# A hybrid decoder trunk on one core: the scheduler's order taken from its detailed timing model instead of its simple one

## The chip, the cores and the metric

The kernel runs on one core of a Trainium2 chip. The metric is device time in microseconds of one execution of the whole program; lower is better. The kernel before was timed three times: 1619.57, 1621.16 and 1629.75 us, so its median is 1621.16 us. The execution that was profiled took 1613.0 us, of which the span from the first to the last instruction is 1610.9 us.

## The reference

One layer of a decoder, applied to a prompt of 2048 tokens and to 8 sequences of 8 new tokens, all in 32-bit floats. In outline:

```python
xn = rms_norm(x, norm_g);  p = xn @ w_in              # 1024 -> 4224 columns
# convolution branch (512 wide): h, bg, cg, gc are columns of p
u = cg * h;  z = causal width-3 convolution of u over positions
y_conv = bg * z * silu(gc)
# RWKV-7 branch (8 heads of 64): r, k, v, low-rank decay and learning-rate inputs, gate
pr = pr + mu_shift * (previous position's pr - pr)
decay = exp(-c * sigmoid(w0 + tanh(wl) @ w_dec2));  a = sigmoid(a0 + al @ w_a2)
kk = normalised(k * k_k);  k = k * (1 + (a - 1) * k_a)
# per token: S = S diag(w) + (S(-kk)) (kk*a)^T + v k^T ;  o = S r
y_rwkv = (group_norm(o) + bonus) * silu(gr)
out = rms_norm(x + concat(y_conv, y_rwkv) @ w_out, final_norm_g)
```

Besides the outputs of both sets of tokens, the last convolution rows, the last normalised row and the final matrix states are returned.

## The kernel before, in words

**Stages.** The prompt is handled in two halves of 1024 tokens; the 64 sample tokens ride along with the first half. Each half first normalises and transposes its rows (`xprep`, lines 211 to 289) and then runs four stages, one for each pair of heads, so there are eight stages (the loop at line 932). After them `out_weights` and `out_tile` (lines 883 to 924) multiply by the output weights and store the result in 17 row blocks.

**A stage.** `rwkv_pair` (line 430) projects the columns r, k, v and the gate of the pair and prepares the operands of the recurrence on VectorE (DVE), ScalarE (ACT) and GpSimd (POOL). `inverse` (line 640) inverts small triangular matrices: the matrices go to DRAM and come back in another layout (`na<-dn`), 31 dependent pairs of DVE operations substitute through them (`subst`, line 614, tiles `sub` and `xi`), the result is stored (`dx<-xi`, line 669) and 12 DMAs bring it back into the tile `AB` (line 678); a DVE transpose (line 680, tile `na`) and small matmuls into the PSUM tile `cx` follow. `wkv` (line 726) then walks through the half in 16 chunks of 64 tokens, each depending on the one before. In a chunk TensorE and DVE take turns: matmuls into `ca`, the copy `xs` (line 741), matmuls into `ca`, the scaling `u` (line 751), matmuls into `cb`, and the new state into `sv` (line 120). `conv_group` (line 329) projects the four column groups of the convolution branch and works on them; it depends on nothing of the recurrence.

**Projections.** Every projection of 128 columns (`project`, line 309) is a series of 24 matmuls for each of three token blocks, all into the PSUM tile `pj`: the weights and the rows are split into a high and a low part (`split`, line 205: a copy on ACT, a subtraction on DVE or POOL), and three products are summed. In the first half the weights are split on POOL (`wl<-wr,wh`) and stored; in the second half they are loaded back split.

**What sets the order.** The kernel is written for a tile framework. The Python code records all instructions, in the order in which the functions are called, with what each one reads and writes. When the context closes, a scheduler replays the recorded instructions on a timing model of the core. Each time an engine comes free in that model, it is given the earliest recorded instruction among those whose inputs and buffers the model holds ready. The order found in this way is written into each engine's queue, and on the chip every engine works through its queue in exactly that order, waiting wherever the next instruction isn't ready. No order is written out by hand; the record order serves as the priority, and because `conv_group` and the next stage's `rwkv_pair` are recorded after `wkv`, their matmuls fill the places at which the model finds the chain of a stage waiting. Buffers of a tile pool are also handed out in the scheduler's order.

The last lines of the kernel open the context and record the program; the timing model is chosen there.

## Time and profile before

| what | us |
|---|---|
| median of three runs | 1621.16 |
| lowest and highest run | 1619.57, 1629.75 |
| the profiled execution: its own time | 1613.0 |
| its span, first to last instruction | 1610.9 |
| TensorE matmul (PE) busy | 1512.1 |
| TensorE weight load (PEld) busy | 1265.4 |
| VectorE (DVE) busy | 1011.3 |
| ScalarE (ACT) busy | 616.2 |
| GpSimd (POOL) busy | 289.6 |

The profile names an instruction by its engine, the line that recorded it, and the tiles that it writes and reads (`out<-in`). Line 129 is the helper that records every matmul and line 117 the one for copies, lines 120 and 123 those for DVE operations on two inputs, so for them the tile tells which step it is. SP is the queue that issues most DMAs. Idle time of an engine is put down to whatever was ready last before the instruction that ended it. PE's ends of matmuls are modelled. PEclk is the granted clock of TensorE as a share of 2.4 GHz: 1.00 is that level, 0.5 is 1.2 GHz, and a value between them is a mean over a stretch with both.

### The profile page before, as it was taken

The page shows a single profiled execution, that of the slowest core. Times are in us where ns is not written, and L with a number is a line of the kernel's source. Part 1 is how long each engine was busy: PE and PEld are TensorE (multiplying, and loading weights), DVE is VectorE, ACT ScalarE, POOL GpSimd, SP SyncE. Part 2 cuts the span into 40 slices and gives each one's busy share as a digit, 9 for nine tenths or more (in the row PEclk, how much of TensorE's full clock was granted, in tenths as well). Part 3 has the DMA queues.
Part 4 walks back from the last instruction along what each step waited for, and adds up shares of the span by engine and source line. Part 5 has one row for each costly group of instructions (what it writes and reads, how often), then busy time and mean ns, then how long its engine had stood idle before and what let it go on. Part 6 is the DMA issues. An engine that isn't in the chain of part 4 may idle for free.

```text
span 1610.9 us, 29335 instructions
## 1 busy us (share of the span) xinstructions
PE 1512.1 (94%) x11088; PEld 1265.4 (79%) x11088; DVE 1011.3 (63%) x3101; ACT 616.2 (38%) x1591; POOL 289.6 (18%) x395
## 2 busy tenths in 40 slices
PE   4999999999999999989999999999999999899997
PEld 4989778887788777877789678877897788567885
DVE  6377458765687458784586358545864578466544
ACT  6443346324542354344541354135313543342221
POOL 3134103311133112320022002200220022000000
PEclk9989999899999998999999899999999999899999
DMA  7323412342043213441124112411241145414441
GB/s 241 118 83 110 137 49 74 108 122 78 20 136 113 95 50 112 140 125 61 36 73 125 42 36 66 135 39 37 77 127 38 34 118 155 133 62 137 143 137 53
DMA packets 121967, 151.90 MB, mean 94 GB/s; under 512 B 62617, under 2 KB 86681, under 8 KB 121826
## 3 DMA queue, kind: packets, MB, share of 16 engines
q1 hardware_dynamic: 107024, 104.53, 21.2%
q0 software_dynamic: 9536, 34.64, 6.8%
q10 hardware_dynamic: 5266, 10.86, 1.9%
q8 instruction: 88, 1.44, 0.4%
q14 instruction: 53, 0.43, 0.1%
HBM read 92.60 MB, written 57.35 MB: 93 GB/s over the span
## 4 chain that ended last, share of the span: by engine, by line
PE 63%; DVE 23%; issue 5%; DMA 5%; ACT 2%; POOL 1%; SPq 1%; ACTq 0%; DVEq 0%; POOLq 0%
PE pj L129 41%; PE ca L129 5%; PE ax L129 5%; DVE sub L123 5%; PE cb L129 4%; DVE xi L123 4%; DVE hp L123 2%; PE oo L129 2%; PE cx L129 2%; DVE hp L120 1%; PE cx L703 1%; DVE bk L123 1%; DVE t L120 1%; DMA dx<-xi 1%; DMA AB<-dx 1%
## 5 line engine op out<-in xcount | busy, mean ns | idle before, releaser
L129 PE MATMUL pj<-xh,wh 128*128 128x384 f32 (+3 forms) x1856 | 655.4, 354 | 18.0 <-DVE hp L123 13.8
L129 PE MATMUL pj<-xl,wh 128*128 128x384 f32 (+3 forms) x1856 | 652.8, 352 | 2.7 <-POOL xl L207 2.1
L129 PE MATMUL pj<-xh,wl 128*128 128x384 f32 (+3 forms) x1856 | 650.9, 351 | 0.8 <-DMA wl<-wsp 0.8
L129 PEld LDWEIGHTS pj<-xh,wh 128*128 128x128 f32 x1856 | 356.7, 192 | 50.1 <-DVE hp L123 11.5
L129 PEld LDWEIGHTS pj<-xl,wh 128*128 128x128 f32 x1856 | 356.8, 192 | 31.7 <-POOL xl L207 3.0
L129 PEld LDWEIGHTS pj<-xh,wl 128*128 128x128 f32 x1856 | 355.8, 192 | 27.3 <-issue 1.7
L117 ACT ACTIVATE tS<-sv,wc 64x64 f32<-64x64 f32 x256 | 88.0, 344 | 114.8 <-DVE sv L120 94.2
L207 POOL TENSOR_TENSOR wl<-wr,wh 128x512 fp32r<-128x512 f32 x66 | 87.8, 1342 | 193.4 <-ACT wh L117 190.0
L120 DVE SCALAR_TENSOR_TENSOR sv<-cb,wc,tS 64x64 f32<-64x64 f32 x240 | 68.0, 283 | 62.6 <-PE cb L129 56.1
L129 PE MATMUL ax<-L,bk 64*128 64x128 f32 x528 | 79.1, 298 | 20.9 <-DVE bk L123 11.2
L129 PEld LDWEIGHTS ax<-L,bk 64*128 64x128 f32 x528 | 66.1, 197 | 37.9 <-issue 23.6
L123 DVE TENSOR_TENSOR sub<-xi,na 128x126 f32<-128x126 f32 (+22 forms) x248 | 81.5, 329 | 16.5 <-DMA na<-dn 9.7
L117 ACT ACTIVATE t<-pj,prm 128x384 f32<-128x384 f32 (+3 forms) x170 | 68.8, 433 | 54.5 <-PE pj L129 53.4
L751 DVE TENSOR_SCALAR u<-ca,Q 128x64 f32<-128x64 f32 x128 | 36.2, 283 | 82.3 <-PE ca L129 82.1
L531 POOL TENSOR_TENSOR bk<-t,t 64x384 f32<-64x384 f32 (+2 forms) x56 | 58.3, 1041 | 155.3 <-ACT t L503 72.9
L123 DVE TENSOR_TENSOR xi<-xi,sub 128x126 f32<-128x126 f32 (+22 forms) x248 | 77.6, 313 | 7.1
L117 ACT ACTIVATE wh<-wr 128x512 fp32r<-128x512 f32 x66 | 40.5, 626 | 92.0 <-PE pj L129 73.1
L129 PEld LDWEIGHTS ca<-sv,L 128*64 128x64 f32 x528 | 43.3, 134 | 37.2 <-DVE sv L120 12.8
L129 PE MATMUL ca<-sv,L 128*64 128x64 f32 x528 | 67.8, 245 | 0.1
L741 DVE COPY xs<-ca 128x64 f32<-128x64 f32 x128 | 28.7, 224 | 60.4 <-PE ca L129 50.6
L298 POOL DMA_DIRECT2D wh<-wsp x33 | 18.6, 565 | 254.1 <-PE pj L129 216.7
L123 DVE TENSOR_TENSOR hp<-pj,hp 128x512 f32<-128x512 f32 (+1 forms) x34 | 23.4, 689 | 62.6 <-PE pj L129 62.2
(207 smaller groups left out, 2057.4 us busy)
## 6 DMA issues: line engine op xcount, KB each, us to landing
wr<-in_w_in SPq DMA_DIRECT2D x66, 256.0 KB, 3.7
wsp<-wh SPq DMA_DIRECT2D x33, 512.0 KB, 3.1
wsp<-wl SPq DMA_DIRECT2D x33, 512.0 KB, 3.5
wh<-wsp POOLq DMA_DIRECT2D x33, 512.0 KB, 3.6
wl<-wsp POOLq DMA_DIRECT2D x33, 512.0 KB, 4.8
hp<-in_x_prompt SPq DMA_DIRECT2D x28, 512.0 KB, 4.1
la<-yd SPq DMA_DIRECT2D x16, 512.0 KB, 4.0
out_y_p<-hp ACTq DMA_DIRECT2D x16, 512.0 KB, 2.6
```

What stands on the lines that cost most here:

```text
L117: act.activation(out=out, in_=in_, func=AF.Copy, scale=scale, bias=bias)
L120: eng.scalar_tensor_tensor(out=out, in0=in0, scalar=scalar, in1=in1, op0=op0, op1=op1)
L123: dve.tensor_tensor(out=out, in0=in0, in1=in1, op=op)
L129: pe.matmul(out, lhsT=lhsT, rhs=rhs, start=start, stop=stop)
L207: eng.tensor_tensor(out=lo, in0=src, in1=hi.bitcast(F32), op=ALU.subtract)
L298: pool.dma_start(out=wh, in_=wsp[col, 0])
L531: pool.tensor_tensor(out=S.bk[bl.i][hs, chs, h, :], in0=ta[hs, a:a + n].rearrange("p (c j) -> p c j", j=64), in1=wi[hs, a:a + n].rearrange ...
L703: pe.transpose(out=pb[:, i, :], in_=S.bk[bi][:, ca + i].rearrange("p a t -> p (a t)"), identity=ident)
L741: dve.tensor_copy(out=xs_, in_=px)
L751: dve.tensor_scalar(out=u, in0=pu, scalar1=S.Q[:, q:q + 1], scalar2=None, op0=ALU.mult)
```

## The change

The context is opened with another argument. The scheduler then replays the recorded instructions on its more detailed timing model instead of the simple one. Nothing else is touched: the recorded instructions, their operands, the pools with their numbers of buffers and the record order are the same. Each engine's queue may hold its instructions in another order, and tiles may be given other buffers of their pool.

```diff
@@ -1017,7 +1017,7 @@
         I[name] = nc.dram_tensor(f"in_{name}", a.shape, mybir.dt.from_np(a.dtype), kind="ExternalInput").ap()
     for name, shape in _OUTS:
         O[name] = nc.dram_tensor(f"out_{name}", shape, F32, kind="ExternalOutput").ap()
-    with tile.TileContext(nc) as tc:
+    with tile.TileContext(nc, schedule_with_timeline_sim=True) as tc:
         trunk_kernel(tc, I, O)
     r = run_bass_kernel_spmd(nc, [arrays], core_ids=[0])
```

## Rows read from the trace of the kernel before

**Rows 1.** The page: span, then busy us of each engine, share, instructions.

```profile
span 1610.9 us, 29335 instructions
PE 1512.1 (94%) x11088; PEld 1265.4 (79%) x11088; DVE 1011.3 (63%) x3101; ACT 616.2 (38%) x1591; POOL 289.6 (18%) x395
```

**Rows 2.** Busy time by stretch: start:end, length, each engine's busy (instructions), PEclk, DMA, GB/s.

```profile
0.00:40.00 40.00, 20.07 (x104) 17.36 (x104) 27.19 (x60) 24.93 (x44) 15.77 (x33) 1.00 0.72 243
...
880.00:920.00 40.00, 34.76 (x372) 28.01 (x371) 12.55 (x46) 11.82 (x37) 3.58 (x8) 0.87 0.29 77
...
1040.00:1080.00 40.00, 37.29 (x391) 29.44 (x389) 14.61 (x58) 12.75 (x39) 3.63 (x8) 0.91 0.27 76
...
1200.00:1240.00 40.00, 36.05 (x385) 28.84 (x383) 13.64 (x51) 12.51 (x39) 3.57 (x8) 0.91 0.29 79
...
900.00:960.00 60.00, 60.00 (x576) 45.22 (x577) 29.91 (x125) 26.86 (x83) 2.61 (x6) 1.00 0.13 42
```

**Rows 3.** Same view, instructions on tile pj alone (PE, PEld, DVE, ACT).

```profile
840.00:885.00 45.00, 40.53 (x254) 39.05 (x253) 5.02 (x10) 2.47 (x6) 1.00 0.41 115
900.00:960.00 60.00, 37.10 (x157) 23.55 (x157) 3.28 (x6) 3.98 (x10) 1.00 0.13 42
```

**Rows 4.** Groups of instructions: busy us, mean ns, then idle before them and releasers.

```profile
L129 PE MATMUL pj<-xh,wh 128*128 128x384 f32 (+3 forms) x1856 | 655.4, 354 | 18.0 <-DVE hp L123 13.8 <-DVE t L120 2.8 <-DMA wh<-wsp 1.3
...
L129 PE MATMUL ax<-L,bk 64*128 64x128 f32 x528 | 79.1, 298 | 20.9 <-DVE bk L123 11.2 <-DVE nwag L120 4.3 <-DVE L L123 3.0
...
L129 PE MATMUL cx<-na,AB 32*32 32x32 f32 x512 | 14.3, 205 | 14.6 <-DVE na L680 14.6
```

**Rows 5.** Timeline, 883 to 892 us: start, duration, instruction, [idle before <-releaser].

```profile
883.12 0.34 PE L129 MATMUL pj<-xh,wl 128*128 128x384 f32 x1
883.30 0.33 PE L129 MATMUL pj<-xh,wh 128*128 128x384 f32 x1
...
884.16 0.34 PE L129 MATMUL pj<-xh,wl 128*128 128x384 f32 x1
889.74 0.64 PE L129 MATMUL cx<-na,AB 32*32 32x32 f32 x16 [5.24 <-DVE na L680]
...
890.80 0.52 PE L129 MATMUL pj<-xl,wh 128*128 128x384 f32 x1
891.12 0.52 PE L129 MATMUL pj<-xh,wl 128*128 128x384 f32 x1
...
882.21 8.46 SPq L678 DMA_DIRECT2D AB<-dx  x12
...
889.38 0.31 DVE L680 STREAM_TRANSPOSE na<-AB 128x128 f32<-128x128 f32 x1 [4.93 <-DMA AB<-dx]
```

**Rows 6.** Timeline, 157 to 164 us, inverse of the first stage.

```profile
157.40 2.74 POOL L207 TENSOR_TENSOR wl<-wr,wh 128x512 fp32r<-128x512 f32 x2 [8.03 <-ACT wh L117]
...
157.40 0.29 DVE L123 TENSOR_TENSOR xi<-xi,sub 128x126 f32<-128x126 f32 x1
157.72 1.28 DVE L123 TENSOR_TENSOR sub<-xi,na 128x130 f32<-128x130 f32 x1
...
163.01 0.69 PE L129 MATMUL pj<-xh,wh 128*128 128x384 f32 x1 [2.45 <-DVE hp L123]
```

**Rows 7.** Timeline, one chunk of the recurrence, 909 to 912.5 us.

```profile
909.13 0.28 DVE L751 TENSOR_SCALAR u<-ca,Q 128x64 f32<-128x64 f32 x1 [0.66 <-PE ca L129]
...
909.68 0.33 PE L129 MATMUL cb<-u,bt 64*64 64x64 f32 x4
...
911.15 0.23 DVE L741 COPY xs<-ca 128x64 f32<-128x64 f32 x1 [0.42 <-PE ca L129]
...
911.85 0.33 PE L129 MATMUL ca<-xs,AB 64*64 64x64 f32 x4
...
912.23 0.28 DVE L751 TENSOR_SCALAR u<-ca,Q 128x64 f32<-128x64 f32 x1 [0.86 <-PE ca L129]
```

**Rows 8.** Group of the chunks' scaling step (idle before it, releaser).

```profile
L751 DVE TENSOR_SCALAR u<-ca,Q 128x64 f32<-128x64 f32 x128 | 36.2, 283 | 82.3 <-PE ca L129 82.1
```

## The prediction, made before the result was known

> **What bounds the kernel now.** I read the page's busy shares first. TensorE is busy 1512.1 of 1610.9 us and the next engine, DVE, 1011.3 [rows 1], so a new order can win only where TensorE stands still, works at the lower clock, or loses time between matmuls. Its idle time is 1610.9 - 1512.1 = 98.8 us. The view by stretches puts 40 - 20.1 = 19.9 us of that into the first 40 us [rows 2], where rows are still being loaded and normalised; any order needs those first transfers, so I leave that part alone. About 79 us remain, some 10 us for each of the eight stages.
>
> Within a stage the stretches differ. In the walk through the chunks TensorE is busy for the whole stretch, 60.00 of 60 us [rows 2], because projection matmuls fill every gap of the chain: 157 of the 576 matmuls in those 60 us write pj [rows 3]. There the plan made with the simple model is already good. The stretches in which a stage passes from the inverse to the chunks lose most: 34.8, 37.3 and 36.1 busy of 40 us, at a mean granted clock of 0.87 to 0.91 [rows 2]. The groups say what TensorE stood before: 14.6 us before the small matmuls of the inverse, 20.9 before `ax<-L,bk`, 18.0 before projections, of which 13.8 waited for DVE to empty a PSUM tile [rows 4].
>
> The timeline of one hand-over is the clearest sign of a wrong plan. At 884.16 TensorE starts a projection matmul in the middle of a series; the next entry in its queue is `cx<-na,AB`, which starts at 889.74 after 5.24 us of idling [rows 5]. That entry waits for the transpose at 889.38, which waits for DMAs that SP issues from 882.21 on over 8.46 us [rows 5]. The interrupted series is resumed right behind it, with operands that had long been there. So the simple model expected the DMAs some 5 us before they landed; a model that gets this right would have put that much projection work ahead.
>
> **The change part by part.** No instruction is added, removed or resized, so every engine's work is the same to first order; what moves is the order in all queues, SP's and POOL's DMA issues included, and the buffers that go with it. Four terms can be priced.
>
> *The hand-over.* If the plan knows when the 12 DMAs land, the 14.6 us before `cx<-na,AB` [rows 4] are filled with projection matmuls. I take all 14.6 (bounds 0 and 14.6). The DMAs themselves stay: SP still needs its 8.46 us, so what is late next is the chain itself.
>
> *The clock behind it.* After the stop, matmuls of 384 columns follow each other at 891.12 - 890.80 = 0.32 us, before it at 883.30 - 883.12 = 0.18 us [rows 5]: the lower level. The three stretches with means of 0.87, 0.91 and 0.91 hold (0.13 + 0.09 + 0.09) x 40 / 0.5 = 25 us at the lower level [rows 2]. Some 12 of the 14.6 us of idling lie in them, so 13 us of work ran there, and 1 - 0.18/0.32 = 44% of that is lost: about 6 us (bounds 0 and 11, all 25 at 44%).
>
> *The wait for DVE to empty pj, 13.8 us* [rows 4]. The case at 163.01 waits 2.45 us [rows 6]. Just before it a DVE step of the substitution took 1.28 us where its neighbour of nearly the same size took 0.29, while POOL was in two operations of 2.74 us together [rows 6]. A plan can only avoid this if its model knows that the two slow each other down. I take 4 of 13.8, a little under a third, between 0 (a plan that doesn't know it) and 13.8. The Trainium skill, in "SBUF — State Buffer", section "Summary: rules for kernel authors", says that a DVE operation with two SBUF inputs and a GpSimd operation that reads SBUF block each other until the first is through. The trace agrees, 1.28 beside 0.29 us; by that rule alone, with POOL's splits needed in the same stretch, this term would be 0 and the sum below 24 us instead of 28.
>
> *The wait before `ax<-L,bk`, 20.9 us* [rows 4]. These matmuls of `rwkv_pair` need operands from a series of DVE, ACT and POOL steps. Part is real latency, part a bad place in DVE's queue (4.3 us of it wait for `nwag`, a step of the normalisation of the stage before). A third, 7 us (bounds 0 and 20.9).
>
> *What is given back.* The matmuls that fill the hand-over no longer cover the chunks. Price of a chunk: from one `u` to the next it takes 912.23 - 909.13 = 3.10 us; in it TensorE starts late by 909.68 - 909.41 = 0.27 us after `u` and by 911.85 - 911.38 = 0.47 after `xs` [rows 7]. Without projections in between I let half of these 0.74 us go: a bare chunk of 2.73 us. The projections of a chunk are 157 x 3.10 / 60 = 8.1, which done densely take 8.1 x 45 / 254 = 1.4 us [rows 3]. So a chunk that loses its cover costs 2.73 + 1.4 - 3.10 = 1.0 us (0.66 if all 0.74 go, 1.4 if none). Filling 14.6 us takes the cover of about ten chunks, 10 us; but the next stage's projections can follow them in, so I charge 4 (bounds 0 and 10).
>
> Sum: 14.6 + 6 + 4 + 7 - 4 = 27.6, say 28 us off the profiled execution's own 1613.0, which makes 1585. That execution stands 8.2 us (0.5%) under the median of 1621.16, so on the median the forecast is **1593 us**. With all terms at their good ends (14.6 + 11 + 13.8 + 20.9 = 60) it is 1561; with their bad ends (-10) 1631.
>
> **The rivals.** *The chunks lose their cover: slower.* The cover is a matter of fine placing: in the chunk above TensorE takes up a step 0.27 to 0.47 us after DVE is done [rows 7]. If the new plan commits longer runs of projections ahead of the chain, or spends them during the inverse, where 254 matmuls ran in 45 us [rows 3], chunks walk bare later. There are 128 chunks [rows 8]; if half of them go bare at 0.66 to 1.0 us each, that is 42 to 66 us, and the time is about 1675. It decides from about 28 / 1.0 = 28 bare chunks on, a fifth of them. For it: TensorE has no idle time in the chunks now, so that stretch can hardly get better; all 79 us lie elsewhere. Against it: both models give the engine to the earliest recorded instruction that is ready, and the chain is recorded ahead of its filling.
>
> *Nothing that can be measured.* The waits before `ax` and for DVE are real latency and contention, the hand-over is won, and a few chunks give it back: 14.6 + 6 - 10 = 11 us, 1610. For it speaks how much of the idle time has DVE behind it, an engine in one queue that shares with POOL; against it the 5.24 us that were plainly misplanned.
>
> *The order does not change where it matters.* If both models agree on every decision on TensorE, the time stays at 1621. The stop at 884 to 889 us speaks against it, since only a model with the same error would plan it again.
>
> **How the numbers follow.** Forecast (faster) 0.45, bare chunks (slower) 0.34, nothing measurable 0.18, same order 0.03. Faster by over 1%, which is 16 us and about what a measurement of this kernel can tell from no change, is the first case: 0.45; within 1% the last two: 0.21; slower 0.34. The forecast's own range is 1561 to 1605. The range for 8 in 10 has to reach across to bare chunks: 1555 leaves out about 0.07 below, where more than the priced terms would have to be won; 1695 is the case in which 74 of 128 chunks go bare at 1.0 us, and leaves out about 0.12 above.
>
> **What would show it.** The hand-over: the group `cx<-na,AB` loses its 14.6 us of idling, with projections running up to it, and the granted clock in the stretches behind the inverse is 1.00. The evacuation: the idle time before `pj<-xh,wh` falls under 13. `ax<-L,bk` falls to some 14. The chunks: the period from one `u` to the next stays near 3.1 us with TensorE busy throughout; if stretches of the chunks show periods near 2.7 us with hardly any pj matmul, or much longer periods with long runs of them, the slower rival holds. The prediction is wrong if TensorE's total idle time does not fall below 80 us, or if it falls and the time does not follow because the busy time between matmuls grew.

## The result and the profile after

The changed kernel takes **1771.14 us** (median of 4 runs, 1762.16 to 1780.17), the kernel before, timed beside it, 1620.37 (4 runs, 1616.09 to 1629.75). The ratio is 1.0922 with an interval of 1.0847 to 1.0997: some 150 us slower, where 1593 was forecast. The profiled execution took 1762.16 us.

The first lines of the page, and the row of the granted clock in 40 slices, answer to [rows 1]:

```profile
span 1760.4 us, 29250 instructions
PE 1571.2 (89%) x11088; PEld 1348.3 (77%) x11088; DVE 1010.1 (57%) x3101; ACT 618.7 (35%) x1591; POOL 290.5 (17%) x395
PEclk9999877997789877999879978997899699996889
```

Each engine has the same count of instructions at work as before, so no work was added. The span grew by 149.5 us: TensorE is busy 1571.2 - 1512.1 = 59.1 us longer with the same matmuls, and idle 189.2 instead of 98.8 us, 90.4 more. The granted clock, averaged over the span, fell from 0.969 to 0.883. With two levels that is (1 - 0.883) / 0.5 x 1760 = 412 us at the lower level, against 100 before. The prediction had named a total idle time that does not fall below 80 us as a sign of being wrong; it rose.

The groups answer to [rows 4], with the two rows of the walk that had no idle time worth a place there (busy us, mean ns, then idle us before them and releasers):

```profile
L129 PE MATMUL pj<-xh,wh 128*128 128x384 f32 (+3 forms) x1856 | 657.4, 355 | 39.5 <-DVE t L120 13.4 <-ACT wh L117 12.0 <-DVE hp L123 5.5
L129 PE MATMUL ca<-sv,L 128*64 128x64 f32 x528 | 87.7, 293 | 25.5 <-DVE sv L120 19.9 <-ACT sv L117 5.5
L129 PE MATMUL ax<-L,bk 64*128 64x128 f32 x528 | 84.7, 292 | 1.8 <-DVE L L123 1.5
L129 PE MATMUL cb<-u,bt 64*64 64x64 f32 x512 | 52.2, 292 | 30.8 <-DVE u L751 30.7
L129 PE MATMUL cx<-na,AB 32*32 32x32 f32 x512 | 12.8, 194 | 2.0 <-DVE AB L694 1.3 <-DVE na L680 0.7
```

Both waits that the forecast lived on are gone: `cx<-na,AB` 14.6 to 2.0, `ax<-L,bk` 20.9 to 1.8. In their place TensorE stands in the walk itself, 30.8 us before `cb<-u,bt` and 25.5 before `ca<-sv,L`, and 39.5 instead of 18.0 before projections. Another 41 us stand before transposes by matmul into `cx` (lines 703, 708, 715, 866 and 876), which had next to none before; the largest of these groups waits for DVE:

```profile
L703 PE MATMUL cx<-cst,bk 128*128 128x128 f32 x132 | 29.9, 340 | 18.9 <-DVE c L120 13.2 <-DVE c L123 3.1 <-DVE AB L694 2.1
```

Where the time lies shows best when the span is cut at the `u` steps (line 751), 16 in each stage. A walk runs from the first to the last `u` of a stage, a passage from there to the next stage's first (worked out from the start times in each profiled execution, us):

| kernel | before first u | 8 walks | 7 passages | after last u | span |
|---|---|---|---|---|---|
| before | 199.1 | 460.2 | 794.7 | 156.9 | 1610.9 |
| changed | 226.1 | 689.0 | 769.9 | 75.5 | 1760.4 |

The walks lost 229 us, the rest of the program won 79. Part of both is a shift: the last walk now holds 284 projections instead of 129 and takes 118.7 us instead of 63.0, and what follows the last `u` is shorter by 81. The other seven walks lost 173 us with fewer projections in them, 802 instead of 988. In the walks TensorE's idle time grew from 0 to 80 us and its time at the lower level from 0 to 314 us; in the passages they fell from 64 to 55 and from 82 to 55.

Stretches of a passage (980 to 1010) and of the walk of the fifth stage, all instructions (columns as in rows 2), answer to the 60.00 of 60 us there:

```profile
980.00:1010.00 30.00, 27.11 (x289) 24.91 (x287) 6.28 (x15) 9.37 (x30) 2.93 (x7) 1.00 0.34 89
1010.00:1030.00 20.00, 16.89 (x167) 13.41 (x164) 8.81 (x45) 6.70 (x19) 0.00 (x0) 0.82 0.00 1
1030.00:1050.00 20.00, 18.47 (x118) 14.88 (x119) 13.02 (x35) 10.24 (x30) 3.00 (x5) 0.67 0.10 29
1050.00:1070.00 20.00, 17.18 (x151) 13.42 (x151) 10.82 (x49) 8.86 (x23) 1.73 (x3) 0.76 0.29 88
1070.00:1095.00 25.00, 23.39 (x160) 19.27 (x161) 16.42 (x38) 7.02 (x19) 3.80 (x7) 0.85 0.05 13
```

The same view, instructions on `pj` alone (PE, PEld, DVE, ACT, clock), answers to [rows 3]:

```profile
980.00:1010.00 30.00, 22.75 (x145) 20.96 (x143) 3.26 (x6) 4.51 (x12) 1.00 0.34 89
1010.00:1030.00 20.00, 4.71 (x24) 4.14 (x24) 0.00 (x0) 0.58 (x1) 0.82 0.00 1
1070.00:1095.00 25.00, 13.93 (x67) 11.81 (x68) 1.21 (x2) 0.88 (x2) 0.85 0.05 13
```

This part of the passage is at the full clock. The stretch at the walk's start holds 24 projections in 20 us, most of them before its first `u` at 1014.20, the last one 67 in 25 us, and between them TensorE's clock is 0.82 down to 0.67. The timeline of that walk, `u` on DVE and the matmul that follows it, answers to [rows 7]:

```profile
1017.61 0.28 DVE L751 TENSOR_SCALAR u<-ca,Q 128x64 f32<-128x64 f32 x1 [0.43 <-PE ca L129]
1017.95 0.33 PE L129 MATMUL cb<-u,bt 64*64 64x64 f32 x4 [0.39 <-DVE u L751]
...
1020.08 0.28 DVE L751 TENSOR_SCALAR u<-ca,Q 128x64 f32<-128x64 f32 x1 [0.43 <-PE ca L129]
...
1022.54 0.28 DVE L751 TENSOR_SCALAR u<-ca,Q 128x64 f32<-128x64 f32 x1 [0.43 <-PE ca L129]
1022.88 0.48 PE L129 MATMUL cb<-u,bt 64*64 64x64 f32 x4 [0.39 <-DVE u L751]
...
1025.91 0.28 DVE L751 TENSOR_SCALAR u<-ca,Q 128x64 f32<-128x64 f32 x1 [0.46 <-PE ca L129]
...
1072.45 0.28 DVE L751 TENSOR_SCALAR u<-ca,Q 128x64 f32<-128x64 f32 x1
...
1081.92 0.28 DVE L751 TENSOR_SCALAR u<-ca,Q 128x64 f32<-128x64 f32 x1
...
1094.93 0.28 DVE L751 TENSOR_SCALAR u<-ca,Q 128x64 f32<-128x64 f32 x1 [2.85 <-PE ca L129]
```

Two kinds of chunk stand where nearly all carried some projections; the chunk of [rows 7] took 3.10 us, the 15 steps from `u` to `u` of that walk 55.3 / 15 = 3.69 in the mean. Bare chunks come first: 2.47 and 2.46 us apart while the matmul on `u` takes 0.33 us, then 3.37 once it takes 0.48, at the lower level of the clock. The last two carry long runs: 9.47 and 13.01 us. Counted over the 120 steps from one `u` to the next within a stage, 79 have no projection at all (before: none), 34 have 13 or more, and before 93 had 5 to 12. The queue of TensorE says the same: the projections stood in 684 uninterrupted runs, 428 of them of 1 to 3 matmuls; they now stand in 306, of which 68 have 9 to 16, 63 have 17 to 23 and 45 more than 23 (before 37, 7 and 27).

The 3.37 against 2.47 isn't the clock alone, because TensorE's matmuls stand in another order in that chunk. The first two walks of the same profile have pairs of bare chunks whose 24 matmuls stand in the same order. `u` in them, first and second walk,

```profile
229.99 0.28 DVE L751 TENSOR_SCALAR u<-ca,Q 128x64 f32<-128x64 f32 x1 [0.43 <-PE ca L129]
232.46 0.28 DVE L751 TENSOR_SCALAR u<-ca,Q 128x64 f32<-128x64 f32 x1 [0.43 <-PE ca L129]
234.93 0.28 DVE L751 TENSOR_SCALAR u<-ca,Q 128x64 f32<-128x64 f32 x1 [0.43 <-PE ca L129]
237.67 0.28 DVE L751 TENSOR_SCALAR u<-ca,Q 128x64 f32<-128x64 f32 x1
...
433.54 0.28 DVE L751 TENSOR_SCALAR u<-ca,Q 128x64 f32<-128x64 f32 x1 [0.58 <-PE ca L129]
436.92 0.28 DVE L751 TENSOR_SCALAR u<-ca,Q 128x64 f32<-128x64 f32 x1 [0.44 <-PE ca L129]
439.96 0.28 DVE L751 TENSOR_SCALAR u<-ca,Q 128x64 f32<-128x64 f32 x1
```

and stretches within these chunks, all instructions:

```profile
230.00:232.40 2.40, 1.74 (x24) 1.31 (x24) 1.07 (x4) 0.83 (x3) 0.00 (x0) 1.00 0.00 0
235.00:237.50 2.50, 1.86 (x24) 1.28 (x24) 1.90 (x12) 1.07 (x3) 0.00 (x0) 1.00 0.00 0
433.60:436.90 3.30, 2.72 (x24) 1.96 (x24) 2.10 (x13) 1.07 (x3) 0.00 (x0) 0.50 0.00 0
437.00:439.90 2.90, 2.41 (x24) 1.93 (x24) 2.39 (x14) 0.69 (x2) 0.00 (x0) 0.50 0.00 0
```

In one order a chunk takes 2.47 us at the full clock (from 229.99) and 3.04 at the lower level (from 436.92), in the other 2.74 (from 234.93) and 3.38 (from 433.54). The lower level costs a bare chunk about 0.6 us.

### The profile page after: what moved, and what is told of

Its sections match the earlier page's. It is cut to its first block, busy times and chain, and to the rows that moved or that the text cites. A ratio compares the mean times of both kernels' runs of the same rounds, so it can differ in the third digit from the quotient of the medians.

```text
span 1760.4 us, 29250 instructions
## 1 busy us (share of the span) xinstructions
PE 1571.2 (89%) x11088; PEld 1348.3 (77%) x11088; DVE 1010.1 (57%) x3101; ACT 618.7 (35%) x1591; POOL 290.5 (17%) x395
## 4 chain that ended last, share of the span: by engine, by line
PE 66%; DVE 19%; DMA 6%; issue 5%; ACT 3%; POOL 1%; SPq 1%; DVEq 0%; POOLq 0%; ACTq 0%
PE pj L129 44%; PE ax L129 5%; PE ca L129 5%; PE cb L129 4%; DVE sub L123 2%; PE oo L129 2%; DVE c L120 2%; DVE xi L123 2%; PE cx L129 2%; DMA na<-dn 1%; DVE sv L120 1%; DVE hp L120 1%; DVE hp L123 1%; DVE u L751 1%; PE cx L866 1%
## 5 line engine op out<-in xcount | busy, mean ns | idle before, releaser
L129 PE MATMUL pj<-xh,wh 128*128 128x384 f32 (+3 forms) x1856 | 657.4, 355 | 39.5 <-DVE t L120 13.4
L129 PE MATMUL pj<-xl,wh 128*128 128x384 f32 (+3 forms) x1856 | 644.4, 347 | 2.7 <-POOL xl L207 2.0
L129 PEld LDWEIGHTS pj<-xh,wh 128*128 128x128 f32 x1856 | 364.8, 197 | 69.7 <-ACT wh L117 13.0
L129 PEld LDWEIGHTS pj<-xl,wh 128*128 128x128 f32 x1856 | 365.5, 197 | 21.4 <-POOL xl L207 2.4
L129 PE MATMUL ca<-sv,L 128*64 128x64 f32 x528 | 87.7, 293 | 25.5 <-DVE sv L120 19.9
L531 POOL TENSOR_TENSOR bk<-t,t 64x384 f32<-64x384 f32 (+2 forms) x56 | 56.5, 1010 | 298.1 <-DVE t L120 190.0
L129 PEld LDWEIGHTS ca<-sv,L 128*64 128x64 f32 x528 | 56.2, 169 | 57.3 <-DVE sv L120 36.1
L129 PEld LDWEIGHTS ax<-L,bk 64*128 64x128 f32 x528 | 66.3, 188 | 19.6 <-issue 16.3
L129 PE MATMUL cb<-u,bt 64*64 64x64 f32 x512 | 52.2, 292 | 30.8 <-DVE u L751 30.7
L123 DVE TENSOR_TENSOR AB<-ax,msk 64x384 f32<-64x384 f32 (+2 forms) x88 | 48.8, 555 | 51.2 <-PE ax L129 50.0
L129 PEld LDWEIGHTS cb<-u,bt 64*64 64x64 f32 x512 | 31.2, 167 | 57.7 <-DVE u L751 46.9
L129 PE MATMUL oo<-sv,L 128*64 128x64 f32 x528 | 75.3, 272 | 0.0
L123 DVE TENSOR_TENSOR xi<-xi,sub 128x126 f32<-128x126 f32 (+22 forms) x248 | 68.5, 276 | 6.4
```

Source lines behind the costliest of these rows:

```text
L123: dve.tensor_tensor(out=out, in0=in0, in1=in1, op=op)
L129: pe.matmul(out, lhsT=lhsT, rhs=rhs, start=start, stop=stop)
L531: pool.tensor_tensor(out=S.bk[bl.i][hs, chs, h, :], in0=ta[hs, a:a + n].rearrange("p (c j) -> p c j", j=64), in1=wi[hs, a:a + n].rearrange ...
```

## The experiments

**The theories.** The main one (A): the plan of the detailed model puts long runs of ready projections ahead of steps of the chain that are about to become ready. A queue works in order, so the chain waits for the run; the run then is missing as filling of later chunks, and bare chunks idle TensorE and run at the lower clock. After the first runs it was widened (A2): the same happens in the queues of the other engines. Rivals were that the other queues alone make the loss, that buffers or waits do, that the bare chunk's latency alone explains it without the clock, and that the chain only lacked priority.

In most kernels an engine's queue is pinned to a stored order after everything is recorded. The edges bind the order of issue on one engine alone and add no wait between engines. In the trace of the first experiment all but 28 of TensorE's 11088 matmuls start at the places of the stored order, the 28 within three places of it. Queues that are not pinned are planned anew around the pinned ones, so they are near those of the named kernel, not equal to them; counted by tiles and lines in the traces, 940 of DVE's 3101 instructions stand at another place than before with runs of 18, 767 with runs of 6, 392 with the stops filled and 18 with the hand-overs filled:

```diff
     with tile.TileContext(nc, schedule_with_timeline_sim=True) as tc:
         trunk_kernel(tc, I, O)
+        pin(tc, nc, ["PE"])
...
+def pin(tc, nc, engines):
...
+                tc.add_manual_dep(made[name], prev, mybir.DependencyInfo(
+                    mybir.DependencyClass.NoSync, mybir.DependencyReason.DATA), reason="pin")
```

All runs together, with the ratio to the kernel before on the same chip, the cut of the profiled execution as above, and the mean granted clock:

| kernel | us | ratio (95%) | walks | passages | clock |
|---|---|---|---|---|---|
| changed | 1771.14 | 1.0922 (1.0847 to 1.0997) | 689 | 770 | 0.883 |
| PE as before | 1699.4 | 1.0478 (1.042 to 1.0535) | 468 | 866 | 0.939 |
| PE, DVE as before | 1646.66 | 1.0166 (1.0052 to 1.0281) | 462 | 831 | 0.957 |
| PE, DVE, ACT as before | 1634.24 | 1.0087 (1.0017 to 1.0156) | 460 | 811 | 0.963 |
| all five queues as before | 1620.73 | 0.998 (0.994 to 1.002) | 460 | 811 | 0.959 |
| simple model, PE as changed | 1839.98 | 1.1355 (1.1277 to 1.1433) | 726 | 800 | 0.855 |
| changed, chunks prioritised | 1771.31 | 1.0931 (1.0857 to 1.1006) | 687 | 778 | 0.877 |
| simple, runs of 6 | 1656.34 | 1.0235 (1.0181 to 1.0289) | 480 | 819 | 0.959 |
| simple, runs of 18 | 1762.0 | 1.0874 (1.0793 to 1.0955) | 564 | 839 | 0.913 |
| simple, all held back | 1836.2 | 1.1337 (1.1299 to 1.1374) | 557 | 885 | 0.831 |
| simple, hand-overs filled | 1621.02 | 1.0018 (0.9985 to 1.005) | 460 | 812 | 0.961 |
| simple, stops filled | 1649.15 | 1.02 (1.0161 to 1.024) | 463 | 826 | 0.956 |

The cut comes from single executions. That of "all five queues" has 811 us of passages where the kernel before has 795, with the same order, so differences of 16 us and less in that column say nothing.

**TensorE's queue put back** in the changed kernel, by the diff above.

> Detailed model, but TensorE's queue is pinned to the order of the kernel before; DVE, ACT, POOL and SP still take their order from the detailed model. Theory A (the loss is TensorE's order: long runs of projection matmuls committed ahead of the chain, then bare chunks): within 2% of 1620, 1590 to 1650 us, chunk chains of a stage back at 55 to 60 us, half-clock time near 100 us. Theory B (the loss is the order of the other queues, the DMAs above all, or the other buffers; TensorE's runs only follow from it): most of the 150 us stay, 1720 us or more.

Measured: 1699.4 us, between the ranges of the two theories. The walks are back at 468 us; with the next experiment, the order of TensorE decides them. But 72 of 150 us came back, not all. The passages grew to 866 us instead, and TensorE stands at the hand-over longer than ever, 28.9 us:

```profile
L129 PE MATMUL cx<-na,AB 32*32 32x32 f32 x512 | 15.2, 212 | 28.9 <-DVE na L680 27.1 <-DVE AB L694 1.8
L680 DVE STREAM_TRANSPOSE na<-AB 128x192 f32<-128x192 f32 (+1 forms) x24 | 8.5, 355 | 39.5 <-DMA AB<-dx 39.2
```

DVE itself stands 39.5 us before the transposes; in the kernel before the same row is

```profile
L680 DVE STREAM_TRANSPOSE na<-AB 128x192 f32<-128x192 f32 (+1 forms) x24 | 8.5, 355 | 13.4 <-DMA AB<-dx 12.9
```

and in the changed one it shows 38.5 too, while it falls to 24.2 with DVE's queue put back as well and to 14.5 with all five. So the other queues' order makes the passage longer, and TensorE only shows it.

**TensorE's queue of the changed kernel under the simple model**: the argument stays off, and `pin` gets the other order.

```diff
     with tile.TileContext(nc) as tc:
         trunk_kernel(tc, I, O)
+        pin(tc, nc, ["PE"])
```

> Simple model, but TensorE's queue is pinned to the order of the changed kernel; the other queues take their order from the simple model. Theory A: about as slow as the changed kernel, 1740 to 1800 us, stages' chains at 80 us or more. Theory B: near the kernel before, 1600 to 1660 us.

Measured: 1839.98 us, slower than the changed kernel and above the range of theory A; the walks take 726 us. TensorE's order is enough for the whole loss, and more: the other queues of the detailed plan fit its TensorE order better than the simple ones do. So the parts do not add up from both ends, and "72 of 150" is a share under one sequence of steps.

**The other queues, one after another**: the same kernel as the first with `["PE", "DVE"]`, then `"Activation"` added, then `"Pool"` and `"SP"`.

> Detailed model, with TensorE's and DVE's queues pinned to the orders of the kernel before; ACT, POOL and SP from the detailed model. The run with TensorE alone pinned left 82 us of loss, about 10 us a stage between the chunks. Theory A2 (every in-order queue of the detailed plan commits ready work ahead of urgent work, DVE's above all, since DVE feeds TensorE): most of the 82 us go, 1620 to 1660 us. Theory B2 (ACT's order, or the order of the DMAs on SP and POOL, makes them): 1680 to 1700 us as before.

> The same with ACT's queue pinned too; only POOL and SP, with the DMAs, take their order from the detailed model. Theory A2: 1615 to 1640 us. If the DMAs' order on SP and POOL is what costs (theory B): still 1680 us or more. If it is ACT: the difference to the run with TensorE and DVE pinned shows it.

> Detailed model with all five queues pinned to the orders of the kernel before. What is left of the change is only the choice of buffers. If buffers matter, some of the loss stays, over 1640 us; if only orders matter, 1605 to 1635 us.

Measured: 1646.66, 1634.24 and 1620.73 us. Putting DVE's queue back wins 53 us, and the intervals of the two ratios lie apart. The last two steps, 12 and 13 us, lie within overlapping intervals, so only their sum, 1.0166 to 0.998, is shown. With all five queues pinned nothing of the change is left but the choice of buffers, and it makes no difference (0.994 to 1.002). So the loss goes with the order. Buffers are handed out in the order of the plan; whether those of the changed kernel's own order cost anything beside it is not separated.

**Priority for the chain** in the changed kernel:

```diff
-                chunk(bl.i, ca + i, cb + bl.ch0 + c, bl.ch0 + c, bt, sv, i, po[:, c], nxt, pc)
+                with tc.high_priority():
+                    chunk(bl.i, ca + i, cb + bl.ch0 + c, bl.ch0 + c, bt, sv, i, po[:, c], nxt, pc)
```

> Changed kernel, with every chunk of the recurrence recorded at raised priority. If the detailed plan commits whatever is ready in long runs before the next step of the chain becomes ready (theory A), priority cannot help: the runs of 17 and more projection matmuls stay and the time is 1720 to 1800 us. If instead the chain loses to work of its own rank or to the next stage's work in the choice between ready instructions (theory C), it recovers: below 1680 us.

Measured: 1771.31 us, and still 78 bare chunks. The plan did change in detail (315 runs of projections instead of 306), the time did not: the walk already stood ahead in the record. That fits a plan in which the chain's step isn't yet ready when the run is committed, and speaks against one in which it is ready and loses to the projections.

**Long runs alone.** Under the simple model, TensorE's queue of the kernel before, but in each walk the projections are gathered into runs of 18, or of 6; each projection stays in its walk.

> Simple model, TensorE's queue pinned to the order of before, with one change: inside the walk through the chunks the projection matmuls are held back until 18 are together and then stand in one run (101 runs of 18; 1963 matmuls moved by at most 17 places of their kind). Same work, same stages. Theory A, length of runs alone: a chunk that meets a run takes about 2.5 + 18 x 0.17 + 0.3 = 6 us or more, the others are bare at 2.5 to 2.7, in the mean 4.1 instead of 3.5 us, so about 75 us over 128 chunks: 1680 to 1710. If the length of runs is harmless and only the supply of filling matters: within 1% of 1620.

> As the run with projection matmuls held back into runs of 18, but in runs of 6 (321 runs, 1969 matmuls moved). If the loss grows with the length of a run (a step of the chain that is ready waits for what is committed ahead of it): between nothing and the 145 us of runs of 18; a run of 6 takes 6 x 0.17 + 0.2 = 1.2 us against a gap of about 0.7 us in the chain, so some 0.3 to 0.5 us for each of 321 runs less the gaps they fill, 20 to 70 us: 1640 to 1690. If any change of the fine order costs as much: 1740 or more.

Measured: 1762.0 and 1656.34 us, 145 and 37 over the kernel before; the first is above its range of 1680 to 1710, which expected 75 us more in the walks, the second within its own. Idle time before the matmul on `u`, in the kernel with 18,

```profile
L129 PE MATMUL cb<-u,bt 64*64 64x64 f32 x512 | 44.4, 249 | 25.9 <-DVE u L751 24.0 <-DVE nwax L123 0.4
```

and in the one with 6:

```profile
L129 PE MATMUL cb<-u,bt 64*64 64x64 f32 x512 | 43.1, 243 | 14.3 <-DVE u L751 13.6
```

The loss grows with the length of the runs, and TensorE's order with runs of 18 costs nearly as much as the whole change. The walks hold nearly the same number of projections, 1117 before, 1111 with runs of 6 and 1121 with runs of 18; what differs is that the chain stands behind a run, and that chunks after it are bare, 32 of the 120 steps with runs of 18 and 1 with runs of 6. With runs of 6 the granted clock is 1.00 in all eight walks, so the 20 us that they lose (480 against 460) are waiting without the clock. With runs of 18 the walks lose 104 us and spend 133 us at the lower level; the passages are longer too (839 us), in part perhaps because the other queues were planned anew.

**All projections of a walk held back** until the next preparation, under the simple model. This was to tell the bare chunk's price from that of the runs: one theory expected a gain in the walks from shorter chunks, the other that the lower clock eats it. Only the fifth, seventh and eighth walk came out bare (at most one projection). In the other five the matmuls return before the last chunk: 106 to 175 of them stand between the late chunks of the walk, nearly all in one block.

> Simple model, TensorE's order of before, but within the walk through the chunks every projection matmul is held back until the next preparation of a pair (about 150 matmuls a stage), so that all chunks are bare and the projections stand behind them; in the last stage the output projections stand behind the walk. If a bare chunk costs only its latency (2.5 us, the clock playing no part): 16 x 2.5 + 150 x 0.17 = 66 us a stage instead of 56, 8 x 10 = 80 us in all, 1690 to 1710. If bare chunks let TensorE's clock fall to 0.5 (3.4 us a chunk in the changed kernel at that level against 2.5 at the full one): 80 us a stage, 180 us in all, 1780 to 1830, with the granted clock near 0.6 in those stretches.

Measured: 1836.2 us, 6 us above the range of the theory with the clock and far from the other. A stretch of the fifth walk, all instructions:

```profile
1033.00:1077.00 44.00, 35.75 (x332) 26.10 (x332) 23.29 (x107) 18.15 (x54) 0.47 (x2) 0.55 0.08 26
```

The same stretch, instructions on `pj` alone (PE, PEld, DVE, ACT, clock):

```profile
1033.00:1077.00 44.00, 0.00 (x0) 0.00 (x0) 0.61 (x1) 0.13 (x1) 0.55 0.08 26
```

and `u` in it, by the timeline:

```profile
1063.32 0.28 DVE L751 TENSOR_SCALAR u<-ca,Q 128x64 f32<-128x64 f32 x1 [0.58 <-PE ca L129]
1066.64 0.28 DVE L751 TENSOR_SCALAR u<-ca,Q 128x64 f32<-128x64 f32 x1 [0.30 <-PE ca L129]
1069.63 0.28 DVE L751 TENSOR_SCALAR u<-ca,Q 128x64 f32<-128x64 f32 x1
1072.62 0.28 DVE L751 TENSOR_SCALAR u<-ca,Q 128x64 f32<-128x64 f32 x1 [0.58 <-PE ca L129]
```

No projection runs, the clock is 0.55, and a chunk takes 3.32, 2.99 and 2.99 us, where the same three took 4.35, 3.70 and 3.85 with their projections. This walk took 51.0 us against 55.3 before, the seventh 51.4 against 55.3 and the eighth 56.4 against 63.0. Taking all its filling away wins a walk 4 to 7 us, and its 129 to 141 projections still have to be done. Where they come back in a block the walk is 12 to 27 us longer than before; the passages take 885 us and the stretch behind the last `u` 38 us more. The matmuls inside the chain, not their cover, get slower: `ca<-sv,L` takes 325 ns in the mean here, 245 with runs of 6 and 293 in the changed kernel.

**Only the hand-overs filled.** The good part of the forecast by itself: simple model, TensorE's queue of the kernel before, with 32, 18 and 25 projections pulled ahead of the first `cx<-na,AB` in the fifth to seventh stage.

> Simple model, TensorE's order of before, but in stages 5, 6 and 7 the 32, 18 and 25 projection matmuls that follow the first small matmul of the inverse are placed ahead of it, so that they fill the stops of 5.24, 2.71 and 3.95 us. The first term of the prediction on its own: 11.9 us of idling and about 6 us of lower clock gone, less what the walk through the chunks lacks of filling (bounds 0 and 10): ratio 0.989 to 0.997. If the filling is only shifted and comes back as bare chunks: 0.998 to 1.003.

Measured: 1621.02 us, ratio 0.9985 to 1.005: nothing. The two matmul groups behind the hand-over in this kernel,

```profile
L129 PE MATMUL cx<-na,AB 32*32 32x32 f32 x512 | 14.8, 209 | 8.4 <-DVE na L680 4.3 <-DVE AB L694 4.1
L129 PE MATMUL cx<-AB,na 32*32 32x32 f32 x512 | 14.8, 209 | 10.3 <-DVE na L687 10.3
```

against the second of them in the kernel before:

```profile
L129 PE MATMUL cx<-AB,na 32*32 32x32 f32 x512 | 13.8, 201 | 1.7 <-DVE na L687 1.6
```

The idle time went down by 6.2 us before the first link and up by 8.6 before the second, 16.3 to 18.7 in all. The projections that fill the stop are those that covered the next links of the same dependent path, PE to ACT to DVE and back.

**All visible stops filled**: as before, for 33 stops of TensorE in front of `ax` and `cx` matmuls, 34.8 us of idling, each with as many following projections as fit into it.

> Simple model, TensorE's order of before, with the next projection matmuls placed ahead of 33 of the stops before small matmuls that the trace of before shows (34.8 us of idling in all, the three hand-overs among them), as many as each stop has room for. If TensorE's stops were a loss that order alone can win back: 34.8 us and some clock, ratio 0.97 to 0.98. If they come back elsewhere, as the small matmuls are on the path and now wait behind the projections: 0.985 to 1.005.

Measured: 1649.15 us, ratio 1.0161 to 1.024: slower, and outside both ranges. In that kernel

```profile
L129 PE MATMUL ax<-L,bk 64*128 64x128 f32 x528 | 80.2, 302 | 22.0 <-DVE L L123 15.8 <-DVE bk L123 3.7 <-DVE Q L515 1.5
```

the wait that was to be filled is as long as before, 22.0 against 20.9 us [rows 4], with another releaser. DVE's and ACT's queues came out in another order too, so why this kernel is slower, and not only level, is not shown. No order tried here beats the kernel before.

## Why the prediction was wrong, by its own steps

**The hand-over (14.6).** The event came: idle time 14.6 to 2.0, clock 1.00 in the stretch. Its price did not. The prediction wrote that the DMAs stay and "what is late next is the chain itself", and yet credited all 14.6 us. Filling the three largest stops alone gains nothing (between 0.15% won and 0.5% lost), because the idle time moves to the next link. Idle time of TensorE on a path that DVE, DMA and ACT set is not time to be had.

**The clock behind it (6).** True for the place, 1.00 in 980 to 1010 us and 55 instead of 82 us at the lower level in the passages, wrong for the kernel: 100 us at the lower level became 412, 314 of them in the walks, where there had been none.

**The wait for DVE to empty pj (4 of 13.8).** The wait for `hp` fell by 8.3 us to 5.5, but new releasers, `t` with 13.4 and `wh` with 12.0, took its place, and the group stands at 39.5. It was a loss of 21.5. The rule on DVE and POOL, from the Trainium skill's "SBUF — State Buffer", "Summary: rules for kernel authors", would have given 0 for this term, as the prediction worked it out; no run here separates it.

**`ax<-L,bk` (7 of 20.9).** 19.1 us of it went, nearly the good end, and again bought nothing that can be seen in the time.

**What is given back (-4): the step that failed.** It supposed that some ten chunks lose their cover, ten at most in the bounds. 79 did, and at the price worked out below that is 99 us instead of 4. The reasoning behind it is in the sentence that was held against the slower rival: "both models give the engine to the earliest recorded instruction that is ready, and the chain is recorded ahead of its filling". That says nothing on what each model holds ready at the instant of the choice, and so nothing against runs of 9 to 23. (That the models differ in this is argued from the runs and from the priority that changed nothing; it isn't shown.)

**The slower rival** had the place, the sign and the marks: "periods near 2.7 us with hardly any pj matmul, or much longer periods with long runs of them" is what the timeline shows, and its 64 bare chunks were near 79. It was given 0.34 and a size that was too small, for three reasons. Its prices came from one chunk: 3.10 us covered [rows 7], where the 120 steps of the kernel before take 460.2 / 120 = 3.84 in the mean, and 2.73 bare, where the 79 bare steps of the changed kernel take 268.5 / 79 = 3.40. The 23 of them with a mean granted clock over 0.75 take 62.7 / 23 = 2.73, the forecast's figure; the other 56 take 205.8 / 56 = 3.67, not all of it the clock's doing, as they lie at other places of the walk. The same 79 steps took 315.5 us before, 3.99 each, and carried 824 projections, which done densely take 824 x 45 / 254 = 146 us [rows 3], 1.85 for each step. So a chunk that loses its cover costs 3.40 + 1.85 - 3.99 = 1.26 us, and not 0.66 to 1.0. Then, it had no price for the chain's wait behind a run; with the bare chunks that come with it, the two kernels with gathered runs show 37 and 145 us. And it spoke of TensorE's queue alone, where the first experiment leaves 79 of 150 us with the other four, 53 of them DVE's. The prediction counted SP's and POOL's DMA issues as moved, but priced none of DVE's.

**The range** ended at 74 bare chunks of 1.0 us each, 1695. At the measured count and price the same sum is 79 x 1.26 = 99 us, or 1720. What it leaves out are the other 41 steps, which carry the runs: they take 420.5 us where the same steps took 144.6, 276 us more for 793 more projections, of which 793 x 45 / 254 = 140 us is the dense price, already in the sum. The other 135 us or so are the chain's wait behind the runs, the lower clock in them and what the other queues add, which the runs don't separate within the changed kernel. Against all this stand the 79 us won outside the walks.

**What stays open.** Why the detailed model holds projections ready and the chain not, so that runs of about 20 come out, isn't in any trace of the chip. The lower clock's share wasn't isolated, since no run kept the clock up with the same order. At about 0.6 us for each of 56 bare chunks it would be some 34 us in them, an estimate from the pairs of chunks above; what it costs in the chunks with runs isn't known.

## What to carry to other kernels

The kernel in which TensorE was busy all through its dependent chain owed that to filling in small doses between the steps (428 of 684 runs were of one to three matmuls); the lengths of runs in the queue told more of the plan than its idle time did. Before idle time is credited, ask which engine's path ends it: if filling comes from a fixed stock, the stop moves to the next link. And a new planner reorders every queue, so price the in-order queue of the second engine as well, and price a bare chain at the lower clock.

## What the runs showed of the hardware

The price of a bare chunk isn't one number: with its matmuls in the same order it takes 2.47 us at the full clock and 3.04 at the lower level, in another order 2.74 and 3.38, and the matmul on `u` 0.33 and 0.48. The clock fell within the row of bare chunks; TensorE had idled 0.33 to 0.39 us ahead of two matmuls of each chunk. In the walk without any filling the granted clock was 0.55 over 44 us with TensorE busy for 35.75 of them, and the 15 steps from `u` to `u` took 51.0 us. With 141 projections between them, at the full clock, they took 55.3: the filling made the walk 4 us longer, where its dense price is 141 x 45 / 254 = 25 us. Not expected either was that TensorE's new order costs more with the other queues planned by the simple model, 1839.98, than with all of them new, 1771.14.
